# Two DeltaNet heads per scan and per substitution, with TensorE's order from an event list

## The chip, the core and the metric

The kernel runs on one core of one Trainium2 chip. The metric is the device time of one execution in microseconds (us). The engines are TensorE (PE, with its weight loads as PEld), VectorE (DVE), ScalarE (ACT), GpSimd (POOL) and SyncE (SP), whose queue issues the DMAs.

## The reference

One layer of a hybrid backbone over 512 latent tokens and 256 context tokens of width 1024: a half-step SwiGLU FFN, a token mixer, a second half-step FFN, a final norm. The mixer has two branches. The pooling branch forms windowed means of four channel groups. The gated DeltaNet branch has 8 heads of 128 channels; q, k and v come from one projection each, then a convolution of five taps over the tokens and SiLU. Each head is scanned in both directions in chunks, each with a decay and a beta of its own:

```python
def gdn_inputs(p, conv_w, a_log, dt_bias):
    qkv = short_conv(p[..., :QKV_END], conv_w).astype(jnp.float32)
    q, k, v = [t.reshape(B, L, GDN_HEADS, GDN_HEAD_DIM) for t in jnp.split(qkv, 3, axis=-1)]
    q = l2norm(q) * GDN_HEAD_DIM ** -0.5
    k = l2norm(k)
...
def gated_delta(q, k, v, beta, g, S0):
    cum = jnp.cumsum(gc, axis=-1)
...
    lmat = jnp.where(strict, jnp.einsum('nbhid,nbhjd->nbhij', kb, kc) * decay, 0.0)
    a_mat = lmat + jnp.eye(CHUNK, dtype=jnp.float32)
    rhs = jnp.concatenate([vb, kb * jnp.exp(cum)[..., None]], axis=-1)
    sol = lax.linalg.triangular_solve(a_mat, rhs, left_side=True, lower=True, unit_diagonal=True)
    aqk = jnp.einsum('nbhid,nbhjd->nbhij', qc, kc) * decay
...
    def step(S, xs):
        u_n, w_n, qd_n, kd_n, aqk_n, bl_n = xs
        v_new = u_n - jnp.einsum('bhcd,bhde->bhce', w_n, S)
        o = jnp.einsum('bhcd,bhde->bhce', qd_n, S) + jnp.einsum('bhij,bhje->bhie', aqk_n, v_new)
        S = S * bl_n[..., None, None] + jnp.einsum('bhcd,bhce->bhde', kd_n, v_new)
        return S, o
```

The latent scans start from the state at the end of the context's scan. The output of each head is normalised, gated and projected; a gated sum of both branches goes through one more projection.

## The kernel before

The kernel goes through four stretches: the first FFN, the pooling branch, the DeltaNet stage, and the merge with the second FFN. Dense products are made in three passes of half-width parts (`hi` and `lo` of weight and activation, line 132 in `job`); all small products take f32 operands directly, which the profile shows as two records for each matmul. Activations lie with channels on the partitions and 768 tokens (512 latent, 256 context) along the free axis, so a projection over both parts takes, for each of 8 input blocks and 3 passes, one matmul of 512 columns and one of 256. `weights` (L107) loads 512 KB of weights on SP's queue and splits them; `bank(tag)` (L51) hands out one of 8 banks of PSUM: 4 of `b` (projections), 2 of `g` (scan), 2 of `a` (the rest).

`head(h)` (L589) makes kf, qf and vf of one head: three `job`s, each followed by `conv_silu` (L567), which copies the projection from PSUM into `raw` with a border, scales the middle tap into `cv`, adds four taps on VectorE (L583) and applies SiLU. `head(0)` is called ahead of the pooling branch (L687), `head(1)` in the line behind it (L732). The pooling branch makes, for 2 halves and 4 token blocks, 24 matmuls of 256 columns into one bank and splits the result; then for 4 groups a window product and a small `job`. 

The DeltaNet stage has three generators a head. `front` (L757) transposes k into `kt` (L764), squares and sums it on ScalarE, transposes q for its norms (L771), and transposes v into `vt`. `invert` (L802) loads 2 rows of accumulated decay, broadcast to all partitions (`crow`, L808), forms exp(-|difference|) with 12 activations a head (L817), multiplies it into k times k (L824) as `L` and into k times q as `aqk`, and inverts the triangular matrices: blocks of 16 by forward substitution on VectorE, 15 steps of a product and a sum (L866) with `transpose`s around it (L872), then in three levels with small matmuls (L881 to L926). `scan` (L938) makes six chained steps, in each both directions of one head: state times k (L952), solve with `L`, state update with `kt` (L985), new state (L994). A step's two directions fill half a bank.

The loop at the end (L1038 on) runs scan of head k, inversion of head k+1 and front of head k+2 beside one another, in the order of letters in `ORDER`; behind each round stand the projections of head k+3, one output gate (`gate`) and a share of the 16 branch gates (`branch_gates`):

```python
    ORDER = "sfifsisiissiis"
    SHARE = (3, 2, 0, 0, 0, 0, 0, 0, 6, 5)
    for k in range(-2, H):
        stages = {c: g(i) for c, g, i in (("s", scan, k), ("f", front, k + 2), ("i", invert, k + 1)) if 0 <= i < H}
        for c in ORDER:
            if c in stages:
                next(stages[c], None)
...
        if k >= -1 and k + 3 < H:
            head(k + 3)
        if 0 <= k + 1 < H:
            gate(k + 1)
```

This text order is not the order of execution: a scheduler at build time orders each engine's instructions by its own estimates, within the data dependences. After the scheduling each engine takes its instructions in the given order.

Of the kernel before, what the change touches and what calls it, by code (L numbers as in the profile page):

```python
# [16 lines left out]
D = 1024  # L17
# [24 lines left out]
def layer_kernel(ctx, tc, a, out):  # L42
# [522 lines left out]
    kf, qf, vf = {}, {}, {}  # L565

    def conv_silu(w, tl, parts, dst, r=None):  # L567
        r = r or job(w, u_hi, u_lo, range(KT), parts)
        raw = pj.tile([128, 776], F32, tag="raw", name="raw", bufs=1)
        cv = pj.tile([128, 772], F32, tag="cv", name="cv", bufs=1)  # L570
        n = 772 if len(parts) == 2 else 512
        tap = [vec[:, 1, 24 * t + tl:24 * t + tl + 1] for t in range(5)]
        pool.memset(raw[:, 0:2], 0.0)
        pool.memset(raw[:, 514:518], 0.0)
        act.copy(out=raw[:, 2:514], in_=r["lat"][:, :512])
        act.activation(out=cv[:, 0:512], in_=r["lat"][:, :512], func=AF.Copy, scale=tap[2])
        if len(parts) == 2:
            pool.memset(raw[:, 774:776], 0.0)
            pool.memset(cv[:, 512:516], 0.0)
            act.copy(out=raw[:, 518:774], in_=r["ctx"][:, :256])  # L580
            act.activation(out=cv[:, 516:772], in_=r["ctx"][:, :256], func=AF.Copy, scale=tap[2])  # L581
        for t in (0, 1, 3, 4):
            dve.scalar_tensor_tensor(out=cv[:, :n], in0=raw[:, t:t + n], scalar=tap[t], in1=cv[:, :n],  # L583
                                     op0=ALU.mult, op1=ALU.add)
        act.activation(out=dst[:, 0:512], in_=cv[:, 0:512], func=AF.Silu)
        if len(parts) == 2:
            act.activation(out=dst[:, 512:768], in_=cv[:, 516:772], func=AF.Silu)

    def head(h):  # L589

        for c0, tl, parts, store, tag, bufs in ((D, 8, BOTH, kf, "kf", 4), (0, 0, ONLY, qf, "qf", 4), (2 * D, 16, BOTH, vf, "vf", 2)):
            store[h] = pj.tile([128, T if len(parts) == 2 else LAT], F32, tag=tag, name=tag, bufs=bufs)
            if h == 0 and c0 == D:
                conv_silu(None, tl, parts, store[h], res_k)
            else:
                conv_silu(weights(w_mix, 0, KT, c0 + 128 * h, EH), tl + h, parts, store[h])
# [135 lines left out]
    head(1)  # L732
# [4 lines left out]
    yg_dram = dr.tile([H, 128, LAT], F32, name="yg_dram")  # L737

# [7 lines left out]
    st = {}  # L746

    def g4(shape, name):
        return mp.tile(shape, F32, tag="g4", name=name, bufs=3)

    def s1(shape, name):
        return mp.tile(shape, F32, tag="s1", name=name, bufs=2)
# [3 lines left out]

    def front(h):  # L757

        kt = mp.tile([128, 6, 128], F32, tag="kt", name="kt", bufs=3)
        ss = mp.tile([128, 10], F32, tag="ss", name="ss", bufs=2)  # L760
        for c0, n in ((0, 4), (4, 2)):
            b = bank("a")
            for c in range(n):
                pe.transpose(b[:, c * 128:(c + 1) * 128], kf[h][:, (c0 + c) * 128:(c0 + c + 1) * 128], ident)  # L764
            act.copy(out=kt[:, c0:c0 + n].rearrange("p c x -> p (c x)"), in_=b[:, :n * 128])
            for c in range(c0, c0 + n):
                sq = mp.tile([128, 128], F32, tag="sq", name="sq", bufs=2)
                act.activation(out=sq, in_=kt[:, c], func=AF.Square, accum_out=ss[:, c:c + 1])
# [499 lines left out]
```

## Time and profile before

| | |
|---|---|
| median of 3 runs | 1755.21 us (1751.45, 1755.21, 1755.26) |
| profiled execution, its span | 1756.71 us, 1755.0 us |
| TensorE busy | 1653.5 us, 94% |
| its weight loads | 1423.9 us, 81% |
| VectorE, ScalarE, GpSimd busy | 1119.0, 842.6, 390.8 us |
| DMA | 183.82 MB, 105 GB/s on the mean |
| granted clock of TensorE, mean | 0.98 of 2.4 GHz |

Times in the rows are us from the span's start. The four stretches: first FFN to about 640, pooling to 722, DeltaNet stage to 1235, merge and second FFN from 1238 on. A row of the timeline names start, duration, engine, line, output, inputs, and in brackets the idle time ahead and what ended it. A group's row has its count, its total and mean duration, and the idle time of its engine ahead of it. TensorE is pipelined, so durations of single matmuls overlap; what a matmul costs is read from the distance of starts in a stretch without gaps.

### The profile page before, as it was taken

To read this page: it belongs to the slowest core of one execution; us is meant where nothing else is said; L and a number is where in the kernel's file an instruction comes from. 1 tells how busy PE (TensorE), PEld (TensorE's weight loads), DVE (VectorE), ACT (ScalarE), POOL (GpSimd) and SP (SyncE) were. 2 spreads that over 40 slices of the span, in tenths; PEclk is the share of its full clock that TensorE was granted. 3 is DMA by queue.
4 is the path that set the end of the run, shared out by engine and by line. 5 is a ranking of instruction groups with operands and counts; after the bars stand their busy time and mean duration, and the time that the engine had idled before them with its cause. 6 is when DMAs were issued, how large, how long until landed. Compare 5 with 4: busy or idle time off the path is not lost.

```text
span 1755.0 us, 31315 instructions
## 1 busy us (share of the span) xinstructions
PE 1653.5 (94%) x12220; PEld 1423.9 (81%) x12220; DVE 1119.0 (64%) x2254; ACT 842.6 (48%) x1851; POOL 390.8 (22%) x493
## 2 busy tenths in 40 slices
PE   6899999999999999889999999999998999999996
PEld 4889898989999778777878788787786788888885
DVE  5778888798888886375678767774555533333333
ACT  5443343434444364667677767665443322222233
POOL 2243444444454121123323331100000000000000
PEclk9999999999999999989999999999999999999998
DMA  9355536361221325532112212224654232333321
GB/s 273 112 155 151 156 96 182 103 189 65 78 67 56 108 82 187 138 100 67 44 52 65 60 45 53 56 61 154 214 158 116 69 98 88 94 96 96 93 64 48
DMA packets 282696, 183.82 MB, mean 105 GB/s; under 512 B 7008, under 2 KB 269877, under 8 KB 282421
## 3 DMA queue, kind: packets, MB, share of 16 engines
q1 hardware_dynamic: 282112, 181.65, 35.6%
q8 instruction: 96, 1.57, 0.4%
q14 instruction: 51, 0.42, 0.1%
q10 hardware_dynamic: 437, 0.18, 0.1%
HBM read 170.22 MB, written 11.58 MB: 104 GB/s over the span
## 4 chain that ended last, share of the span: by engine, by line
PE 71%; DVE 14%; ACT 5%; DMA 5%; POOL 2%; issue 2%; SPq 0%; ACTq 0%; POOLq 0%; DVEq 0%
PE b L132 22%; PE b L345 9%; PE a L132 6%; PE g L132 6%; PE a L345 5%; PE g L345 5%; DVE cv L583 2%; PE b L279 2%; PE a L279 1%; PE g L279 1%; PE a L708 1%; ACT din L848 1%; DVE wlo L120 1%; DMA bg_dram<-bgate 1%; PE b L150 1%
## 5 line engine op out<-in xcount | busy, mean ns | idle before, releaser
L188 ACT CAST fhi<-fst 128x512 fp32r<-128x512 f32 (+1 forms) x136 | 77.7, 605 | 249.6 <-PE b L132 85.6
L132 PE MATMUL b<-hhi,whi 128*128 128x512 f32 (+1 forms) x528 | 187.6, 384 | 0.0
L132 PE MATMUL b<-hlo,whi 128*128 128x512 f32 (+1 forms) x528 | 187.5, 383 | 0.0
L132 PE MATMUL b<-hhi,wlo 128*128 128x512 f32 (+1 forms) x528 | 186.9, 384 | 0.0
L179 POOL TENSOR_TENSOR rs<-rs,mhalf 128x4 f32<-128x4 f32 (+2 forms) x13 | 13.6, 1045 | 665.3 <-DVE rs L177 649.7
L189 DVE TENSOR_TENSOR flo<-fst,fhi 128x512 fp32r<-128x512 f32 (+1 forms) x136 | 87.3, 671 | 92.6 <-ACT fhi L188 92.4
L119 ACT CAST whi<-stg 128x512 fp32r<-128x512 f32 x146 | 89.4, 620 | 91.6 <-PE b L132 59.9
L119 ACT CAST whi<-qst 128x512 fp32r<-128x512 f32 (+1 forms) x160 | 81.6, 512 | 106.5 <-PE b L345 43.2
L119 ACT CAST whi<-qs 128x512 fp32r<-128x512 f32 (+1 forms) x120 | 59.5, 512 | 115.2 <-POOL qs L309 76.2
L583 DVE SCALAR_TENSOR_TENSOR cv<-raw,vec,cv 128x772 f32<-128x772 f32 (+1 forms) x96 | 101.6, 1058 | 11.6 <-ACT cv L581 8.3
L120 DVE TENSOR_TENSOR wlo<-qst,whi 128x512 fp32r<-128x512 f32 (+1 forms) x160 | 100.7, 639 | 10.1 <-ACT whi L119 10.0
L132 PEld LDWEIGHTS b<-hlo,whi 128*128 128x128 f32 x528 | 94.0, 190 | 14.8
L132 PEld LDWEIGHTS b<-hhi,whi 128*128 128x128 f32 x528 | 94.0, 190 | 14.8
L132 PEld LDWEIGHTS b<-hhi,wlo 128*128 128x128 f32 x528 | 93.3, 190 | 14.8
L308 POOL TENSOR_TENSOR qs<-qst 128x512 f32<-128x512 f32 (+1 forms) x40 | 46.4, 1161 | 247.2 <-DMA qst<-in_ffn_w_in_dram 76.6
L120 POOL TENSOR_TENSOR wlo<-stg,whi 128x512 fp32r<-128x512 f32 x46 | 65.4, 1430 | 90.6 <-ACT whi L119 70.6
L120 DVE TENSOR_TENSOR wlo<-stg,whi 128x512 fp32r<-128x512 f32 x100 | 68.2, 686 | 22.1 <-ACT whi L119 20.2
L188 ACT CAST ahi<-q 128x384 fp32r<-128x384 f32 x74 | 37.5, 512 | 75.4 <-DVE q L257 35.6
L120 DVE TENSOR_TENSOR wlo<-qs,whi 128x512 fp32r<-128x512 f32 (+1 forms) x80 | 49.0, 613 | 32.6 <-ACT whi L119 32.6
L132 PE MATMUL b<-xlo,fhi 128*128 128x512 f32 x160 | 63.4, 396 | 0.0
L132 PE MATMUL b<-xhi,flo 128*128 128x512 f32 x160 | 63.4, 396 | 0.0
L132 PE MATMUL b<-xhi,fhi 128*128 128x512 f32 x160 | 63.4, 396 | 0.0
(512 smaller groups left out, 4909.8 us busy)
## 6 DMA issues: line engine op xcount, KB each, us to landing
stg<-in_w_ada_dram SPq DMA_DIRECT2D x56, 512.0 KB, 4.0
stg<-in_w_mix_in_dram SPq DMA_DIRECT2D x49, 512.0 KB, 3.7
fst<-in_ffn_w_in_dram SPq DMA_DIRECT2D x44, 512.0 KB, 3.6
qst<-in_ffn_w_in_dram SPq DMA_DIRECT2D x40, 512.0 KB, 3.4
qst<-in_ffn_w_out_dram SPq DMA_DIRECT2D x40, 256.0 KB, 2.6
adx<-in_w_ada_dram SPq DMA_DIRECT2D x16, 512.0 KB, 6.4
fst<-in_ffn_w_out_dram SPq DMA_DIRECT2D x16, 512.0 KB, 3.9
crow<-cumd SPq DMA_DIRECT2D x16, 384.0 KB, 7.8
```

The costliest lines, as they stand in the source:

```text
L119: (first.copy if first is act else first.tensor_copy)(out=hi[:, :n], in_=w)
L120: second.tensor_tensor(out=lo[:, :n], in0=w, in1=hi[:, :n], op=ALU.subtract)
L132: pe.matmul(res[p][:, :m], lhsT=ww(i), rhs=hh(k)[:, o:o + m], start=(i == 0 and j == 0), stop=(i == n - 1 and j == 2))
L150: pe.matmul(b[32 * j:32 * j + 32, e * 128:(e + 1) * 128], lhsT=sc[:, k, :], rhs=stg[:, k, :], start=(i == 0), stop=(i == 1))
L188: act.copy(out=hi, in_=src)
L189: dve.tensor_tensor(out=lo, in0=src, in1=hi, op=ALU.subtract)
L279: pe.matmul(x, lhsT=ww(k), rhs=rhs(j, part, k), start=n + e == 0, stop=n + e == len(ks) + 1)
L308: pool.tensor_tensor(out=s1, in0=a21, in1=a22, op=ALU.add)
L345: pe.matmul(o, lhsT=ww[:, k], rhs=rhs(j, part, k), start=first and k + i == 0, stop=k + i == nh + 1, skip_group_check=not first)
L583: dve.scalar_tensor_tensor(out=cv[:, :n], in0=raw[:, t:t + n], scalar=tap[t], in1=cv[:, :n], op0=ALU.mult, op1=ALU.add)
L708: pe.matmul(r[:, :256], lhsT=hh[:, k, t * 128:(t + 1) * 128], rhs=ww[:, k], start=n == 0, stop=n == 3 * KT - 1)
L848: act.copy(out=din[o:o + 32, :, 0:12].rearrange("p f u -> p u f"), in_=L[o:o + 32, :, o:o + 32])
```

## The change

Heads are taken in four pairs. Each part of the stage is a generator that yields what it is about to use before it emits it: the engine, a cost in us written into the source, the buffers ("tokens") that it takes, and the events that it waits for. `run` keeps a clock for each engine and, of all threads, takes the one that could start first by these costs; what is emitted in that order is the kernel. On TensorE each instruction of the stage is kept behind the one emitted before it (`InOrder`); the other engines' instructions are still ordered by the scheduler.

What is computed in a pair at once: one substitution for both heads (24 matrices in the place of 12 in the same `[128, 32, 32]` tile), and one scan of six steps with two heads and two directions, which fill a bank. The products around the substitution stay per head. `L` and `aqk` of a head are written to DRAM (`l_dram`, `aq_dram`); each scan step loads its four 128 by 128 pieces back on SP's queue. The convolution reads the projection from PSUM, in two pieces, into its destination; `raw` and `cv` go. The norms of k are a wide square and a reduction on VectorE; those of q a wide square and four matmuls with a column of `ones`. Of a decay row, GpSimd forms the difference, and ScalarE takes Abs and Exp of 768 columns at once. `vt` is scaled on ScalarE. The call `head(1)` behind the pooling branch goes: head 1's projections are the first of the list's. Branch gates, output gates and projections are jobs of one `projections` thread with the lowest priority, whose weights are loaded ahead by two further threads.

```diff
-    def conv_silu(w, tl, parts, dst, r=None):
...
+    def conv_steps(tl, parts, r, dst):
+        tap = [vec[:, 1, 24 * t + tl:24 * t + tl + 1] for t in range(5)]
+        spans = [(r[p], PARTS[p][0], PARTS[p][1]) for p in parts]
+        def tap_of(x, o, n, t):
+            i0, i1 = max(0, 2 - t), n - max(0, t - 2)
+            d = dst[:, o + i0:o + i1]
+            dve.scalar_tensor_tensor(out=d, in0=x[:, i0 + t - 2:i1 + t - 2], scalar=tap[t], in1=d, op0=ALU.mult, op1=ALU.add)
+        for x, o, n in spans:
+            yield "act", n, lambda: act.activation(out=dst[:, o:o + n], in_=x[:, :n], func=AF.Copy, scale=tap[2])
...
-    head(1)
...
+    l_dram = [dr.tile([128, 12, 128], F32, name=f"l_dram{h}") for h in range(H)]
+    aq_dram = [dr.tile([128, 8, 128], F32, name=f"aq_dram{h}") for h in range(H)]
...
+    class InOrder:
+        def __getattr__(self, name):
+            return lambda *args, **kw: tc.keep_in_program_order(getattr(self.engine, name)(*args, **kw))
+    pe = InOrder(pe)
+    TOKENS = {"b": 4, "g": 2, "a": 2, "kf": FB["kf"] - 1, "qf": FB["qf"] - 1, "vf": FB["vf"] - 1, "kt": 4, "vt": 4, "dec": 3,
+              "L": 2, "g4": 3, "s1": 2, "tn": 1, "low": 1, "rv": 3, "S": 2, "ls": 2, "aqs": 1, "ot": 1, "yo": 2,
+              "sgate": 2, "stg": 2, "whi": WB, "wlo": WB}
...
+    def run():
+        while threads:
+            can = [(t, th["prio"], i) for i, th in enumerate(threads) for t in [start_of(th)] if t is not None]
+            t, _, i = min(can)
...
+    MM, TR = 0.2, 0.1
+    def projections():
...
+            for k in range(KT):
+                yield "pe", 0.69 + 0.36 * (len(parts) - 1), tags, (("w", j["name"], k // 4 * 4),)
+                hi, lo = j["w"][k // 4]
+                for e, (ww, hh) in enumerate(((hi, u_hi), (hi, u_lo), (lo, u_hi))):
+                    for p in parts:
+                        pe.matmul(r[p][:, :m], lhsT=ww[:, k % 4], rhs=hh(k)[:, o:o + m],
+                                  start=k + e == 0, stop=k + e == KT + 1)
...
+            spawn(j["then"](r), 0.5)
+    def qkv_job(h, i):
...
+        def then(r):
+            for e, n, emit in conv_steps(tl + h, parts, r, store[h]):
+                yield e, dcost(n) + 0.06 if e == "dve" else acost(n) + (0.06 if e == "act" else 0.0)
+                emit()
+                if e == "dve":
+                    last = state["end"]
+            done(f"{tag}{h}")
+            for _ in parts:
+                free_at["b"].append(last)
...
     def front(h):
+        for c0, n in ((0, 4), (4, 2)):
+            yield "pe", n * TR, ("a",)
...
+            yield "act", acost(n * 128)
             act.copy(out=kt[:, c0:c0 + n].rearrange("p c x -> p (c x)"), in_=b[:, :n * 128])
+            yield "act", acost(n * 128), ("yo",)
+            act.activation(out=sq[:, :n], in_=kt[:, c0:c0 + n], func=AF.Square)
+            yield "dve", dcost(n * 128)
+            dve.tensor_reduce(out=ss[:, c0:c0 + n], in_=sq[:, :n], axis=AX.X, op=ALU.add)
...
+    def front_q(h):
+        act.activation(out=sq, in_=qf[h], func=AF.Square)
         b = bank("a")
         for c in range(4):
-            pe.transpose(b[:, c * 128:(c + 1) * 128], qf[h][:, c * 128:(c + 1) * 128], ident)
+            pe.matmul(b[:, c:c + 1], lhsT=sq[:, c * 128:(c + 1) * 128], rhs=ones[:, 0:1])
...
+    def decay(h, d):
+        yield "sp", 0.05, ("dec",), ((f"own{h // 2 * 2 - 1}",) if h > 1 else ())
+        t = st[h]["dec", d] = mt([128, 6, 128], "dec", 3)
+        sp.dma_start(out=t, in_=cum_rows[d, h].partition_broadcast(128))
+        yield None, 3.5
+        yield "pool", 2.0
+        pool.tensor_tensor(out=t, in0=t, in1=bc(own, [128, 6, 128]), op=ALU.add)
+        yield "act", acost(768)
+        act.activation(out=tf, in_=tf, func=AF.Abs)
+        yield "exp", acost(768)
+        act.activation(out=tf, in_=tf, func=AF.Exp, scale=-1.0)
+        done(f"dec{h}{d}")
...
+    def substitution(p):
+        dve.transpose(out=au[:, 0:1024], in_=s["din"].rearrange("p a b -> p (a b)"))
...
+        dve.transpose(out=T_, in_=ti[:, 0:1024].rearrange("p (x y) -> p y x", y=32))
+        done(f"sub{p}")
+    def after(h):
...
+        yield "sp", 0.05
+        sp.dma_start(out=l_dram[h], in_=L)
+        give("L", 3.5)
+        done(f"inv{h}", 4.0)
+    def operands(p):
+        for s_ in range(6):
+            yield "sp", 0.1, ("ls",), evs
+            t = pair[p]["ls", s_] = mt([128, 2, 2, 128], "ls", 2)
+            for e in range(2):
+                sp.dma_start(out=t[:, e], in_=l_dram[2 * p + e][:, cf:6 + cb + 1:6 + cb - cf])
+            if s_ >= 2:
+                yield "sp", 0.1, ("aqs",)
...
+            done(f"ops{p}{s_}", 3.5)
+    def scan(p):
+        spawn(operands(p), 0)
+        UN = [(e, d) for e in range(2) for d in range(2)]
...
+                yield "pe", 4 * MM, ("g",)
+                for e, d in UN:
+                    pe.matmul(un(b, e, d), lhsT=kf[hs[e]][:, chunk[d] * 128:(chunk[d] + 1) * 128], rhs=S[:, e, d])
...
+            yield "pe", 4 * MM, ("g",), (f"ops{p}{s}",)
+            for e, d in UN:
+                pe.matmul(un(b, e, d), lhsT=ls[:, e, d], rhs=R[:, e, d] if s > 0 else vt[e][:, chunk[d]])
...
+    for p in range(H // 2):
+        for i in range(3):
+            for h in (2 * p, 2 * p + 1):
+                if h:
+                    qkv_job(h, i)
...
+    for p in range(H // 2):
+        spawn(pair_work(p), 2)
+    spawn(scans(), 0)
+    spawn(projections(), 6)
+    run()
```

## Rows read from the trace of the kernel before

**Rows 1.** page, part 1: engine, busy us (share of the span), number of instructions
```profile
PE 1653.5 (94%) x12220; PEld 1423.9 (81%) x12220; DVE 1119.0 (64%) x2254; ACT 842.6 (48%) x1851; POOL 390.8 (22%) x493
```

**Rows 2.** windows by stretch, columns in the first line
```profile
core 0: us, PE busy (x) PEld busy (x) DVE busy (x) ACT busy (x) POOL busy (x), PEclk, DMA share, GB/s
719.00:1238.00 519.00, 486.04 (x5454) 404.99 (x5452) 344.36 (x815) 356.66 (x928) 127.77 (x234) 0.99 0.28 76
...
1480.00:1520.00 40.00, 40.00 (x172) 32.15 (x171) 13.09 (x20) 8.48 (x15) 0.00 (x0) 1.00 0.32 94
...
692.00:702.00 10.00, 10.00 (x88) 10.00 (x88) 4.60 (x8) 1.75 (x4) 0.27 (x4) 1.00 0.21 55
...
745.70:752.30 6.60, 3.02 (x14) 3.02 (x15) 0.09 (x1) 5.26 (x25) 0.00 (x0) 0.50 0.56 144
```

**Rows 3.** timeline of TensorE at 923: start, us, engine, line, out<-in, records
```profile
922.80 1.06 PE L824 MATMUL a<-kf 128*128 128x128 f32 x8
923.69 0.61 PE L952 MATMUL g<-S,kf 128*128 128x128 f32 x4
```

**Rows 4.** timeline of TensorE at both ends of the stage
```profile
704.61 0.28 PE L132 MATMUL b<-hlo,whi 128*128 128x256 f32 x1
...
719.11 0.60 PE L764 MATMUL a<-ident,kf 128*128 128x128 f32 x4
...
722.40 0.39 PE L132 MATMUL g<-dh,pwl 128*128 128x512 f32 x1
...
1234.58 0.40 PE L132 MATMUL b<-hhi,wlo 128*128 128x512 f32 x1
...
1238.26 0.79 PE L132 MATMUL b<-yphi,whi 128*128 128x512 f32 x1 [3.28 <-ACT yphi L188]
```

**Rows 5.** TensorE groups by shape, 719 to 1238: busy us, mean ns, idle
```profile
L132 PE MATMUL b<-hhi,wlo 128*128 128x512 f32 x334 | 137.7, 412 | 0.0
...
L132 PE MATMUL b<-hlo,whi 128*128 128x256 f32 x96 | 29.5, 307 | 0.0
...
L952 PE MATMUL g<-S,kf 128*128 128x128 f32 x160 | 26.6, 289 | 5.6 <-DVE S L994 5.1 <-DVE tm L866 0.5
...
L881 PE MATMUL a<-tr,low 32*32 32x32 f32 x768 | 14.9, 235 | 4.8 <-DVE tr L872 4.7
...
L926 PE MATMUL a<-x,U 64*64 64x64 f32 x96 | 7.3, 222 | 0.0
```

**Rows 6.** waits of TensorE, 719 to 1238: total us, number, longest
```profile
PE a L771 <- ACT kt L765: 9.0, 1, 9.0
...
PE g L952 <- DVE S L994: 5.1, 6, 1.2
...
PE g L985 <- DVE vw L976: 3.8, 2, 2.0
```

**Rows 7.** window of line L132 alone: PE, PEld busy (records), PEclk, DMA share, GB/s
```profile
656.60:719.00 62.40, 29.97 (x142) 23.39 (x141) 0.97 0.51 166
```

**Rows 8.** DMA issues: queue, number, KB each, median us from issue to landing
```profile
crow<-cumd SPq DMA_DIRECT2D x16, 384.0 KB, 7.8
...
yg_dram<-y SPq DMA_DIRECT2D x8, 256.0 KB, 2.2
```

**Rows 9.** timeline of SyncE's queue and ScalarE, 726 to 750
```profile
727.37 1.01 SPq L808 DMA_DIRECT2D crow<-cumd  x2
...
735.81 1.86 ACT L817 ACTIVATE arg<-crow,ncumc 128x128 f32<-128x128 f32 x6 [4.03 <-DMA crow<-cumd]
```

**Rows 10.** ScalarE and VectorE groups by shape, 719 to 1238
```profile
L817 ACT ACTIVATE arg<-crow,ncumc 128x128 f32<-128x128 f32 x96 | 30.8, 398 | 7.0 <-DMA crow<-cumd 7.0
...
L872 DVE STREAM_TRANSPOSE tr<-ti 128x1024 f32<-128x1024 f32 x8 | 15.9, 1991 | 0.0
...
L866 DVE TENSOR_TENSOR tm<-au,ti 128x126 f32<-128x126 f32 x16 | 4.5, 284 | 0.2
...
L583 DVE SCALAR_TENSOR_TENSOR cv<-raw,vec,cv 128x772 f32<-128x772 f32 x52 | 62.2, 1197 | 8.4 <-ACT cv L581 8.0
```

More of the change, by code (lines that the diff above doesn't have):

```diff
@@ L589, in head @@
-    def head(h):
[L591 to L596, printed above, removed]
+    FB = {"kf": 5, "qf": 4, "vf": 2}
@@ new lines, in layer_kernel, with give, done, spawn @@
+    state = {"end": 0.0, "table": None}
+    events = {}
+    threads = []
+    def give(tag, after=0.0):
+        free_at[tag].append(state["end"] + after)
+    def done(name, after=0.0):
+        events[name] = state["end"] + after
+    def spawn(gen, prio):
+        th = {"gen": gen, "prio": prio, "t": state["end"], "last": "pe"}
+        threads.append(th)
+        step(th)
+    def step(th):
+        try:
+            w = next(th["gen"])
+        except StopIteration:
+            threads.remove(th)
+            return
+        th["want"] = (w[0], w[1], w[2] if len(w) > 2 else (), w[3] if len(w) > 3 else ())
@@ new lines, in start_of @@
+    def start_of(th):
+        e, cost, tags, evs = th["want"]
+        unit = "act" if e in ("exp", "silu") else e
+        t = th["t"] + (AFTER[th["last"]] if th["last"] and unit != th["last"] else 0.0)
+        for ev in evs:
+            if ev not in events:
+                return None
+            t = max(t, events[ev] + 0.2)
+        for tag in set(tags):
+            if len(free_at[tag]) < tags.count(tag):
+                return None
+            t = max(t, sorted(free_at[tag])[tags.count(tag) - 1])
+        return max(t, clock[unit]) if e else t
@@ L820, in invert, with before @@
+    def before(h):
+        s, p, e = st[h], pair[h // 2], h % 2
+        for d in range(2):
+            spawn(decay(h, d), 3)
+        yield None, 0.0, ("L",), (f"front{h}", f"dec{h}0", f"dec{h}1")
+        L = s["L"] = mt([128, 12, 128], "L", 2)
+        dec = [s["dec", d] for d in range(2)]
         for c0, n in ((0, 4), (4, 2)):
+            yield "pe", n * MM, ("a",)
             b = bank("a")
@@ L1055, in layer_kernel, with head_work, pair_work @@
-    assert not extra
+        give("yo", 2.5)
+        done(f"out{h}")
+    def head_work(h):
+        for g, prio in ((front(h), -1), (front_q(h), 1), (front_v(h), 2), (before(h), -1)):
+            spawn(g, prio)
+        yield None, 0.0, (), (f"front{h}",)
+    def pair_work(p):
+        if p:
+            yield None, 0.0, (), (f"din{2 * p - 1}",)
+        spawn(cleared(p), -1)
+        for h in (2 * p, 2 * p + 1):
+            spawn(head_work(h), -1)
+        yield None, 0.0, (), (f"din{2 * p}", f"din{2 * p + 1}", f"unit{p}")
+        spawn(substitution(p), -1)
+        for h in (2 * p, 2 * p + 1):
+            yield None, 0.0, (), (f"sub{p}",)
+            spawn(after(h), -1)
@@ L1056, in layer_kernel @@
+    gate_job(H - 2)
+    gate_job(H - 1)
+    for m in range(2 * KT):
+        branch_job(m)
+    for tag in ("kf", "qf", "vf"):
+        events[f"{tag}0"] = 0.0
+    for p in range(H // 2):
+        spawn(pair_work(p), 2)
+    spawn(scans(), 0)
+    spawn(projections(), 6)
+    run()
+    for h in range(H):
+        assert f"out{h}" in events
+    act, dve, pool, pe = engines
     mp_cm.__exit__(None, None, None)
```

669 lines of the change are left out of this document (472 added, 197 removed).

## The prediction

> **What bounds the kernel now.** I read the page's busy times first, then the windows by stretch, the groups of TensorE by shape inside the stretch that the change touches, its waits, and last the timeline at both ends of that stretch. The page says TensorE 94% busy [rows 1], but a matmul's end is modelled, so I count instructions instead. In the second FFN, where nothing interrupts it, 172 matmuls of 512 columns take 40.00 us, 0.2326 us each; in the pooling stretch 88 of 256 columns (and a few of 512) take 10.00 us, some 0.114 us each, and I use 0.1165, half of the former [rows 2]. Eight records of f32 matmuls of 128 columns take 923.69 - 922.80 = 0.89 us, 0.111 us a record [rows 3].
>
> The change touches the DeltaNet stage. Pooling's last matmul starts at 722.40, the first transpose of `front` at 719.11; the stage's last projection matmul starts at 1234.58, ends 0.23 later, and the merge begins at 1238.26 after a wait for ScalarE [rows 4]. In 719 to 1238 the groups hold 1001 matmuls of 512 columns (three groups of about 334, one shown) and 288 of 256 (three of 96): 232.8 + 33.6 us. Twelve groups of f32 matmuls and transposes (32 to 160 records, the largest shown) have 1088 records, 120.8 us. Seven groups of 32- and 64-row matmuls (L881 is the largest, L926 the smallest) are busy 75.8 us [rows 5]. That is 463 us; with some missing records I take 465. From 719.1 to 1234.8 are 515.7 us, so TensorE lacks work for about 51 us, a tenth. The stage is bound by TensorE; no other engine is near (VectorE 344, ScalarE 357, GpSimd 128 of 519 us [rows 2]). The waits say where part of the 51 us is: 9.0 once for `kt` at the start, 5.1 for the new state, 3.8 for `vw` [rows 6]; the rest is many short ones.
>
> A rule speaks for far more room. The weight loads are busy 405 of 519 us, 78% [rows 2]. The Trainium skill (Perfetto Trace Analysis, Identifying the Most-Contended Engine) calls matmul busy time a bad measure of headroom and weight-load busy time a good one. By that, some 114 us would be open here, and the sum below could fall by more than 60 us; but in the uninterrupted FFN stretch the same share is 32.15 of 40, 80%, so here the count decides and the trace does not bear the rule out.
>
> **The change part by part.**
>
> *TensorE's work.* The scan has the same matmuls for two heads in one bank instead of one head's in half a bank: 48 a head before and after. The substitution's small matmuls stay per head. Only the norms of q change: four transposes a head (one record each) become four f32 matmuls with `ones` (two records each): 8 x 4 x 0.111 = 3.6 us more. So none of the 465 us goes away; the change can win only from the 51 us of waiting.
>
> *Head 1 leaves pooling's shadow.* Before, head 1's three projections stand outside the stage and fill TensorE while pooling waits for its copies: L132 has 142 matmuls in 656.6 to 719 [rows 7], of which 5 finish head 0's v and 9 are pooling's own; the other 128 are head 1's k, q and v (72 of 512 and 48 of 256 columns, 16.7 + 5.6 us) and 8 of a branch gate (1.9), together 24.2 us. The blocks between two pooling products are such a filling, as the one at 704.61 [rows 4]. After, head 1 is in the event list, and every TensorE instruction of the list is kept behind the one traced before it, the first behind pooling's last matmul. Pooling's own chain (a copy, eight products, a copy) does not get shorter without the filling, so these 24.2 us move behind 722.6. From below this costs nothing if pooling ends that much earlier, from above 24.2; I take 24.2, since in the trace the products resume as soon as the copy is done.
>
> *Start of the list.* The second batch of k's transposes is listed after the first batch's copy, square and reduction, and the projections stand behind it: some 3 us idle. The first decay rows are counted with 3.5 us in the list; the row load lands after 7.8 us [rows 8], and before, ScalarE waited 4.03 us for it after the issue at 727.37 [rows 9]. The first score matmul waits behind it, and all fill listed later waits too, since TensorE takes no other order: 4 us, between 0 and 9 (the present wait [rows 6]). I take 7 us for the start against the present 9 and more, which goes because head 1's projections fill it.
>
> *Steady state.* Without the start the 51 us leave some 40 us of short waits, 8%. For the change: the substitution runs once for a pair, so of VectorE's 8 transposes of 1991 ns 4 go, with 4 each of the two shorter ones, and half of the 240 little products and sums of some 0.26 us, 31 us (one group of them shown) [rows 10]; ScalarE loses the 96 activations of 398 ns [rows 10] against 32 wide ones, and the tap copies of the convolution (the taps, 1.2 us for 772 columns now [rows 10], read PSUM in two pieces); 24 chained scan steps take the place of 48. Against it: the list fixes the order by written-in costs, and where a copy or a load is later than listed, TensorE stands though other work is ready. The projection loop's banks are held until the last tap is done. I bound the waits by 8% of 492 us (40) and 2% (10) and take 20, near half of the present 8%, as both other busy engines are relieved.
>
> *Through DRAM.* L goes out in one DMA of 768 KB a head and comes back step by step, 80 loads on SP's queue in all, behind which weight loads queue, and the step's solve product waits for them. The trace has a 256 KB write with 2.2 us and the 384 KB rows with 7.8 [rows 8]; so 2.2 to 7.8 us each way. The pair's chain has projections of the next pairs to hide it as long as these last (290 us of them); I count nothing, and up to 4 x 8 = 32 us if the cover is gone. The Trainium skill (DMA: Bandwidth & Descriptors, Anatomy of one DMA) gives a fixed 2 us or so per transfer, nearly all of it the receipt of the last write, which by its formula makes 3.8 us for 768 KB; the 2.2 us row agrees with it, the 7.8 us row does not.
>
> *Clock.* After the 9 us wait the granted clock is 0.50 in 745.7 to 752.3 [rows 2], the 1.2 GHz level. Pooling without its filling has idle stretches of 2 to 11 us; a stretch at that level of the length shown costs 3.3 us. I count it into the 7 us and keep 3 us for the range. The Trainium skill (TensorE: Matmul & The Clock Gate, HAM oscillation) warns of idle gaps between short bursts in the same sense; by it (an estimate) pooling would end 2 to 4 us later.
>
> *Sum.* Start 722.6; work 465 - 1.2 (pooling's last five) + 24.2 + 3.6 = 491.6; start 7; waits 20; the gap to the merge 3.4 as now: 722.6 + 491.6 + 7 + 20 + 3.4 = 1244.6, against 1238.3: 6.3 us later. What follows is unchanged. The profiled execution has a span of 1755.0 us and took 1756.7; the median of the three runs is 1755.2. The sum is made on the span, which is the median within 0.2 us: **1761.5 us**.
>
> **The rivals.**
>
> *The list orders so well that waits nearly vanish (faster).* Waits of 2% (10 us) with a start of 3: 1244.6 - 14 = 1230.6, 7.7 us earlier, 1747. With no wait at all 1217.6, 1734, is the floor. For it: the list's cost of a projection step, 0.69 us, is that of three matmuls of 0.2326, and the chains have slack. It decides from 18 us of waiting in all downwards.
>
> *TensorE stands behind late operands (slower).* One mechanism: a fixed order meets a DMA or a VectorE queue later than listed. The second head of each pair needs a row load after the first one's scores; 7.8 against 3.5 us is 4.3 us, four times 17, and DRAM reads behind SP's queue as much again: 1761.5 + 17 to 34 = 1778 to 1795. Against: other work of the list lies between.
>
> *The order isn't pinned where it matters.* If head 1's projections still run in pooling's shadow, 24.2 us come back: 1737.
>
> *The counted f32 work is itself waiting.* The 197 us of f32 and small matmuls are counted at the rate they show; if a third of that were latency that wider batches hide, the stage would shrink by 60 us: 1700. For it: the rule above of the Trainium skill (Perfetto Trace Analysis, Identifying the Most-Contended Engine), which would find its room here. Against: the eight records of [rows 3] follow each other without a wait at that rate.
>
> **How the numbers follow.** Forecast (20 to 40 us of start and waits, 1754 to 1774) 0.47; nearly no waits 0.25; standing behind operands 0.20; not pinned 0.05; latency in the f32 work 0.03. A measurement tells 0.3%, 5.3 us, from no change. Faster takes the second, fourth and fifth cases less a little, 0.31; same is the lower half of the forecast's band and the upper edge of the second, 0.26; slower is the other half and the third, 0.43. The range leaves 0.1 on each side: 1737 to 1788; the forecast's own is 1754 to 1774.
>
> **What would show it.** Right: between pooling's first product and its last, TensorE has idle blocks of some 2 us where L132 stood, and L132 begins after pooling's last matmul; in the stage the same counts of records; the merge starts near 1245. VectorE's L872-like transposes number 4. Wrong: projections inside pooling's stretch; a waiting total (515.7 us against the counted work) over 45 or under 18 us; a rate of the f32 records other than 0.111 us; waits of TensorE that name the L or score tiles from DRAM.

## The result and the profile after

The changed kernel takes 1838.48 us (median of 4 runs, 1835.82 to 1839.63), the kernel before 1754.66 beside it: ratio 1.0479, 95% interval 1.0461 to 1.0498. Forecast were 1761.5 us, with 1737 to 1788 as the range. The direction was right; the loss is 84 us where the forecast had 6.

First the page's busy times, then the windows of the profiled execution (span 1837.9 us), cut where pooling's last product and the merge's first start; columns as in [rows 1, 2].

```profile
PE 1667.6 (91%) x12252; PEld 1450.2 (79%) x12252; DVE 1089.5 (59%) x2187; ACT 780.8 (42%) x1515; POOL 401.8 (22%) x432
```

```profile
640.00:721.40 81.40, 60.83 (x326) 52.22 (x326) 32.53 (x79) 37.14 (x50) 4.38 (x10) 0.79 0.41 130
721.40:1321.40 600.00, 513.99 (x5609) 446.01 (x5607) 328.21 (x746) 303.91 (x613) 148.51 (x191) 0.90 0.35 102
...
800.00:820.00 20.00, 7.64 (x413) 7.14 (x415) 11.21 (x26) 4.14 (x10) 4.61 (x10) 0.50 0.11 29
1321.40:1837.90 516.50, 495.48 (x2114) 396.66 (x2114) 209.93 (x330) 166.94 (x291) 2.01 (x2) 0.98 0.34 100
```

The whole loss lies in the DeltaNet stage. Behind the merge 516.5 us are left, and before they were 1755.0 - 1238.3 = 516.7; ahead of 721.4 nothing was lost in sum. The stage takes 600.0 us in the place of 515.9 (722.4 to 1238.3, [rows 4]). TensorE is busy 514 us of it, about 31 more than before, and idle 86, where [rows 2] show 519.0 - 486.0 = 33 for nearly the same stretch. VectorE and ScalarE are less busy than before, with 328 and 304 us against 344 and 357; GpSimd is busier, with 149 against 128, and far from full.

What TensorE waits for in the stage, as in [rows 6] (total, times, longest), and the groups that carry the added work, as in [rows 5]:

```profile
PE a L760 <- DVE tr L1157: 30.9, 3, 17.3
PE a L760 <- issue: 15.5, 12, 2.1
PE b L132 <- ACT yphi L188: 7.5, 1, 7.5
PE g L760 <- DVE S L1362: 6.4, 1, 6.4
PE g L760 <- DMA ls<-l_dram: 5.5, 4, 3.0
```

```profile
L760 PE MATMUL b<-hhi,whi 128*128 128x512 f32 x360 | 158.1, 439 | 0.0
...
L760 PE MATMUL b<-hhi,whi 128*128 128x256 f32 x112 | 32.4, 289 | 2.8 <-DVE kf L576 2.8
...
L760 PE MATMUL a<-tr,low 32*32 32x32 f32 x768 | 14.8, 244 | 37.4 <-DVE tr L1157 30.9 <-issue 6.5
...
L760 PE MATMUL a<-ones,yo 128*128 128x1 f32 x64 | 7.9, 244 | 0.8 <-ACT yo L1008 0.7
```

Line 760 is the wrapper that pins TensorE's order, so every instruction of the stage bears it. Three groups of 360 are 1080 matmuls of 512 columns (1001 before), three of 112 are 336 of 256 (288 before). The wait for the transposes behind the substitution (`tr`) was 4.7 us for eight heads [rows 5]; it is 30.9 for four pairs.

The largest wait, on five queues (start, duration, engine, line, output and inputs, and what the engine waited for):

```profile
783.12 0.39 SPq L1042 DMA_DIRECT2D dec<-cumd  x1
...
791.49 1.48 POOL L1046 TENSOR_TENSOR dec<-dec,ncumc 128x768 f32<-128x768 f32 x1 [6.66 <-PE b L760]
...
786.16 0.69 ACT L578 ACTIVATE qf<-b,vec 128x512 f32<-128x512 f32 x1
793.00 0.84 ACT L1049 ACTIVATE dec<-dec 128x768 f32<-128x768 f32 x1 [6.16 <-POOL dec L1046]
...
788.10 0.26 DVE L1147 TENSOR_TENSOR tm<-au,ti 128x110 f32<-128x110 f32 x1
788.28 0.74 DVE L576 SCALAR_TENSOR_TENSOR kf<-b,vec,kf 128x510 f32<-128x510 f32 x1
788.95 0.26 DVE L1150 TENSOR_TENSOR ti<-ti,tm 128x110 f32<-128x110 f32 x1
...
799.06 0.75 DVE L576 SCALAR_TENSOR_TENSOR qf<-b,vec,qf 128x510 f32<-128x510 f32 x1 [4.43 <-ACT qf L578]
...
806.96 1.86 DVE L1157 STREAM_TRANSPOSE tr<-ti 128x1024 f32<-128x1024 f32 x1
...
791.29 0.38 PE L760 MATMUL a<-ident,kf 128*128 128x128 f32 x2
808.96 2.44 PE L760 MATMUL a<-tr,low 32*32 32x32 f32 x133 [17.30 <-DVE tr L1157]
```

VectorE alternates a step of the substitution (L1147, L1150) with a tap of a convolution (L576). The list has the 30 small steps and the two transposes behind them in one piece, 15 x (0.28 + 0.27) + 1.25 + 2.0 = 11.5 us by its written-in costs (14 with the transpose ahead of them and what stands between); here they go from 781.87 to 808.82, 27 us. Into this falls a standstill: a decay row is issued at 783.12 and GpSimd adds to it at 791.49 (the bracket names a TensorE matmul as what ended that wait; that it was the row is read from its issue 8.4 us before, where the stage's rows take a median of 7.0), ScalarE stands 6.16 us in front of it, and the tap scaling behind it (`qf`, L578) holds VectorE for 4.43. TensorE, whose next instruction in the list is the product behind the substitution, waits 17.3 us, and then works at a granted clock of 0.50 from 800 to 820.

### The profile page after: what moved, and what is told of

It is laid out like the page before. It is cut to its first block, busy times and chain, and to the rows that moved or that the text cites. A ratio compares the mean times of both kernels' runs of the same rounds, so it can differ in the third digit from the quotient of the medians.

```text
span 1837.9 us, 31100 instructions
## 1 busy us (share of the span) xinstructions
PE 1667.6 (91%) x12252; PEld 1450.2 (79%) x12252; DVE 1089.5 (59%) x2187; ACT 780.8 (42%) x1515; POOL 401.8 (22%) x432
## 4 chain that ended last, share of the span: by engine, by line
PE 74%; DVE 10%; DMA 6%; ACT 4%; issue 3%; POOL 2%; SPq 1%; POOLq 0%; ACTq 0%; DVEq 0%
PE b L132 13%; PE b L760 13%; PE b L345 8%; PE a L132 6%; PE g L132 6%; PE g L345 5%; PE a L345 5%; PE a L760 5%; PE g L760 4%; PE b L279 2%; DMA dec<-cumd 2%; PE a L706 1%; PE a L279 1%; PE g L279 1%; DVE xT L437 1%
## 5 line engine op out<-in xcount | busy, mean ns | idle before, releaser
L760 PE MATMUL b<-hhi,whi 128*128 128x512 f32 x472 | 172.3, 404 | 2.8 <-DVE kf L576 2.8
L760 PE MATMUL b<-hlo,whi 128*128 128x512 f32 x472 | 159.5, 377 | 0.0
L760 PE MATMUL b<-hhi,wlo 128*128 128x512 f32 x472 | 159.2, 376 | 0.0
L760 PEld LDWEIGHTS b<-hhi,wlo 128*128 128x128 f32 x472 | 83.7, 194 | 16.7
L760 PEld LDWEIGHTS b<-hhi,whi 128*128 128x128 f32 x472 | 84.2, 196 | 15.3 <-issue 3.3
L760 PEld LDWEIGHTS b<-hlo,whi 128*128 128x128 f32 x472 | 84.5, 196 | 12.8
L877 POOL TENSOR_TENSOR wlo<-stg,whi 128x512 fp32r<-128x512 f32 x37 | 47.6, 1286 | 182.9 <-ACT whi L872 182.4
L872 ACT CAST whi<-stg 128x512 fp32r<-128x512 f32 x90 | 55.1, 617 | 70.1 <-PE b L760 61.5
L877 DVE TENSOR_TENSOR wlo<-stg,whi 128x512 fp32r<-128x512 f32 x53 | 36.2, 687 | 63.3 <-ACT whi L872 63.2
L437 DVE SCALAR_TENSOR_TENSOR xT<-q,eff,xT 128x128 f32<-128x128 f32 (+2 forms) x100 | 64.1, 661 | 0.1
L132 PE MATMUL b<-xhi,flo 128*128 128x512 f32 x160 | 63.4, 396 | 0.0
L132 PE MATMUL b<-xlo,fhi 128*128 128x512 f32 x160 | 63.4, 396 | 0.0
L132 PE MATMUL b<-xhi,fhi 128*128 128x512 f32 x160 | 63.4, 396 | 0.0
```

Source lines behind the costliest of these rows:

```text
L132: pe.matmul(res[p][:, :m], lhsT=ww(i), rhs=hh(k)[:, o:o + m], start=(i == 0 and j == 0), stop=(i == n - 1 and j == 2))
L437: dve.scalar_tensor_tensor(out=r[:, o0:o1], in0=c[i][j][:, o0 - j * n2:o1 - j * n2], scalar=gate(m + i, s), in1=r[:, o0:o1], op0=ALU.mult, ...
L760: return lambda *args, **kw: tc.keep_in_program_order(getattr(self.engine, name)(*args, **kw))
L872: act.copy(out=hi, in_=stg[:, i:i + 4])
L877: eng.tensor_tensor(out=lo, in0=stg[:, i:i + 4], in1=hi, op=ALU.subtract)
```

## The experiments

Theory A: the change pins TensorE to the list's order and leaves VectorE, ScalarE and GpSimd to the scheduler, and the two orders don't fit. Theory B: the list has 3.5 us for a decay row that takes 7 to 8, and all queues stand behind it. Theory C is on the waits that the profile puts down to `issue`; D and E ask whether TensorE's work or the chain of pairs sets the pace. All times are medians, with the kernel before at 1752.8 to 1756.3 beside them.

**Orders.** Every engine in the list's order, and none:

```diff
-    pe = InOrder(pe)
+    act, dve, pool, pe = (InOrder(e) for e in (act, dve, pool, pe))
```


> Theory A (two orders): TensorE follows the event list, but VectorE, ScalarE and GpSimd follow the scheduler, which mixes the substitution with convolution taps, so that it takes 27 us where the list has 14; with every engine kept in the list's order the waits of 17.3 and 11.5 us for the transposes behind the substitution fall to under 3 and the time to 1795 to 1810. Theory B (late decay rows): the list believes in 3.5 us for a row load that takes 7 to 8, and ScalarE's queue stands behind it; keeping more engines in the list's order changes nothing on that or makes it worse: 1830 to 1855.

Measured 1805.57 (1802.94 to 1806.57), 33 less than the changed kernel. The second kernel only takes the line `pe = InOrder(pe)` out:

> The list's order as text order only, TensorE free. Theory A: the scheduler's orders fit each other again, TensorE's waits of over 0.3 us sum to 35 to 55 us instead of 85: 1785 to 1805. Theory B: the row loads are as late for the scheduler's own order, the 6 us waits of ScalarE for them stay and TensorE has no more work ready than now: 1825 to 1840.

Measured 1789.31 (1784.12 to 1797.94). In the first, VectorE's order and TensorE's wait, and the waits of the stage:

```profile
794.96 0.19 DVE L760 TENSOR_TENSOR tm<-au,ti 128x30 f32<-128x30 f32 x1
795.48 3.07 DVE L760 STREAM_TRANSPOSE tr<-ti 128x1024 f32<-128x1024 f32 x2
...
798.70 1.54 PE L760 MATMUL a<-tr,low 32*32 32x32 f32 x80 [3.01 <-DVE tr L760]
```

```profile
PE a L760 <- issue: 14.8, 13, 2.1
PE g L760 <- DMA ls<-l_dram: 10.8, 4, 4.8
...
PE a L760 <- DVE tr L760: 4.9, 2, 3.0
```

The wait for `tr` falls from 30.9 to 4.9 us, as A has it. Which engine is it? TensorE pinned with one other:

```diff
-    pe = InOrder(pe)
+    dve, pe = InOrder(dve), InOrder(pe)
```
The other run has `act` in the place of `dve`.

> TensorE and VectorE in the list's order, ScalarE and GpSimd in the scheduler's. Theory A as first told (VectorE's mixing of substitution and taps is the mismatch): most of the 33 us that pinning all engines gave, 1803 to 1815. Theory B: ScalarE's place behind the decay rows is it: 1825 to 1845.

> TensorE and ScalarE in the list's order, VectorE and GpSimd in the scheduler's. Theory A as first told: the waits for the transposes behind the substitution stay at 25 to 35 us, 1828 to 1845. Theory B: 1803 to 1818.

Measured 1838.58 and 1833.19: neither alone gives much, 5.3 us at most. With VectorE pinned the substitution runs in one piece, and ScalarE still stands in front of the decay row:

```profile
801.98 3.05 DVE L760 STREAM_TRANSPOSE tr<-ti 128x1024 f32<-128x1024 f32 x2
...
803.42 0.84 ACT L1049 ACTIVATE dec<-dec 128x768 f32<-128x768 f32 x1 [6.53 <-POOL dec L1046]
```

The waits of the whole stage tell the two causes apart. First come ScalarE's waits for decay rows (`dec`) in the changed kernel, then both waits with VectorE pinned, both with ScalarE pinned, and ScalarE's with all pinned:

```profile
ACT dec L1049 <- POOL dec L1046: 50.0, 11, 7.8
...
ACT dec L1049 <- POOL dec L1046: 55.6, 12, 7.4
PE a L760 <- DVE tr L760: 3.5, 1, 3.5
...
ACT dec L760 <- POOL dec L1046: 11.0, 3, 8.2
PE a L760 <- DVE tr L1157: 27.4, 3, 13.2
...
ACT dec L760 <- POOL dec L760: 11.4, 5, 7.5
```

Each of the two runs takes most of one wait away, keeps the other, and gains little; with all pinned both are small, and 33 us are gone. With VectorE pinned TensorE's idle time in the stage does fall, from 86 to 592.6 - 522.2 = 70 us, but its busy time is 8 us longer and the stage starts 5 us later (726.4); the waits for L, the output and the state are 7.7, 7.0 and 6.5 us for 4.1, 3.7 and 6.4. So "VectorE's mixing" as first told fell, and so did ScalarE's standing in front of decay rows on its own: with no engine pinned ScalarE waits 45.5 us for rows, TensorE 2.9 for `tr`, and the time is 1789. What stays of A is that the engines' orders must fit each other. Whether three engines without GpSimd would do wasn't tried.

**Late rows.** The listed latency 3.5 becomes 9.0, in the changed kernel and with all engines pinned:

```diff
-        yield None, 3.5
+        yield None, 9.0
         yield "pool", 2.0
```


> Only the listed latency of the decay rows changes, 3.5 to 9 us. Theory A: the mixing on VectorE stays, so the waits for the transposes stay within 5 us: 1825 to 1840. Theory B: ScalarE's waits of 6 to 7.5 us for a decay row go, and with them the wait of 6.4 for the new state and most of the 17.3: 1805 to 1818.

> All engines in the list's order, the decay rows listed with 9 us in the place of 3.5. Theory B, now where the list sets every order: ScalarE and GpSimd no longer stand in front of a row, 5 to 15 us less, 1790 to 1800. Rival: the row loads are late but not on the path, and the first pair starts later: 1803 to 1820.

Measured 1856.43 (18 more than the changed kernel) and 1818.18 (1803.29 to 1821.72, 13 more than with all pinned). The first doesn't test B: ScalarE's order is the scheduler's, and its waits for rows stay at 49.5 us. The second does: they fall from 11.4 to 0.7 us, and nothing is gained. With the runs above, B as the main cause fell.

**Head 1's projections** stand ahead of the stage again, with TensorE pinned, with none, with all. The list then has one buffer fewer of `kf`, `qf` and `vf`:

```diff
+    head(1)
     mp_cm = tc.tile_pool(name="mp", bufs=1, reuse_waits="tile")
...
-                if h:
+                if h > 1:
                     qkv_job(h, i)
...
```


> Head 1's three projections stand again ahead of the stage, where they can run beside pooling; the list begins with both heads of the first pair made. The prediction's term: 24.2 us of TensorE's work leave the stage, 1810 to 1818. Rival: pooling's own chain grows by as much, or the first pair waits elsewhere: 1828 to 1840.

> The list as text order only, and head 1's projections ahead of the stage. If TensorE's work bounds the stage when its order is the scheduler's, the 24.2 us of the prediction come back here: 1789 - 24 = 1765 (1760 to 1772). If waits decide as in the pinned order, 1782 to 1792.

> All engines in the list's order, head 1's projections ahead of the stage. Theory D: with orders that fit, TensorE's work bounds the stage, so the 22.3 us of matmuls that leave it come off: 1805.6 - 22 = 1783 (1776 to 1790). Theory E: the chain of pairs (substitution, products around it, scan) sets the pace and TensorE's work is fill, as the 2 us of the same edit with mixed orders say: 1798 to 1810.

Measured 1836.09, 1820.77 and 1785.05. With TensorE alone pinned the stage has 72 matmuls of 512 and 48 of 256 columns fewer and nothing is gained: TensorE idles 101 us in it for 86, with 27.2 us for `tr` and 16.9 for the state. With none pinned the projections went into pooling's shadow anyway, and yet the time is 31 us longer; the list is another one, and no run separates what else it does. With all pinned 20.5 us come off, as D has it; the nudged list below shows why one such difference isn't enough.

**Runs of tiny matmuls.** Between two blocks of 96 records of 32-row matmuls the list must place a projection step (a token that `apart` gives back after a step, or after 3 us without one); first with all pinned, then with head 1 outside too:

```diff
-        yield "pe", 1.9, ("a",)
+        yield "pe", 1.9, ("a", "apart")
+        spawn(apart(), 7)
...
```


> All engines in the list's order, and after each block of 96 records of 32-row matmuls at least one step of a projection before the next such block. Theory C (a long run of tiny matmuls outruns what feeds TensorE with instructions): the 14.8 us of waits for nothing that the profile shows fall to under 4, the time by 8 to 15 us to 1790 to 1798. Rival: these waits are semaphores that the profile doesn't resolve; they stay, 1800 to 1812.

> All engines in the list's order, head 1 outside, and a projection step between two blocks of tiny matmuls. Theory C (runs of tiny matmuls outrun their supply): the 14.4 us of waits for nothing in the profile fall to under 5 and are not given back now that orders fit: 1785 - 9 = 1776 (1770 to 1780). Rival: the second head's products come later and the pair with them: 1781 to 1792.

Measured 1802.55 and 1811.31. The waits called `issue` fall from 14.8 to 6.0 and from 14.4 to 8.7 us. They were to fall under 4 and 5, but the direction bears C out on what makes them. The time doesn't follow: the second head's products come later, and waits for `tr` (12.0 and 12.7) and for L from DRAM (13.9 in the latter) take their place.

**SyncE's queue** in the list's order too, with all pinned and head 1 outside, without and with the blocks apart:

```diff
-    engines = act, dve, pool, pe
+    engines = act, dve, pool, pe, sp
+    sp = InOrder(sp)
```


> As the run with all engines in the list's order and head 1 outside, and SyncE's queue in the list's order too. Theory A in its widest form (any queue in another order than the list costs): the waits for loads and for ScalarE's splits of weights go, 1770 to 1780. Rival: a queue in the list's order stands behind stores whose data come late, and weight loads behind them: 1785 to 1800.

> Both together. If each takes off what its theory says, 1760 to 1772; if the list itself is what is left, 1775 to 1795. Under 1750 it would beat the kernel before.

Measured 1802.79 and 1824.86, 18 and 40 more than the 1785 us of the kernel with all pinned and head 1 outside. Nothing is gained, so A in its widest form has no support here; the times lie above the rival's 1785 to 1800 and the combination's 1760 to 1795 too, and no run shows that late stores cause them.

**How far can an edit of the list be read?** In the kernel of 1785 us every listed VectorE cost gets 0.01 us more; in another the listed costs that the traces contradict are mended:

```diff
-        return 0.2 + 0.00095 * n
+        return 0.21 + 0.00095 * n
```

```diff
-    MM, TR = 0.2, 0.1
+    MM, TR = 0.228, 0.1
...
-        yield None, 3.5
-        yield "pool", 2.0
+        yield None, 7.3
+        yield "pool", 1.5
...
-            done(f"ops{p}{s_}", 3.5)
+            done(f"ops{p}{s_}", 5.0)
```


> All engines in the list's order and head 1 outside (1785 us), and one written-in cost changed by almost nothing: every listed VectorE operation is 0.01 us longer. If an edit of the list does what it says, 1783 to 1787. If the list is a greedy order that any change shuffles, the time jumps by as much as in the runs with blocks apart, 10 us or more either way.

> As the run with all engines in the list's order and head 1 outside, with the three listed costs that the traces contradict: an f32 matmul 0.228 in the place of 0.2, a decay row 7.3 in the place of 3.5 (GpSimd's addition 1.5 in the place of 2.0), the loads of a scan step 5.0 in the place of 3.5. If false costs are what is left of the waits, 1765 to 1778; if the list scatters whatever it is told, anything from 1775 to 1815.

Measured 1801.87 (1798.22 to 1813.62) and 1811.67. An edit that says nothing costs 17 us: the greedy list falls into another order, and any single difference of under some 17 us between two lists shows nothing on its cause. This is one nudge, so the scatter may be larger; the two kernels with none pinned are 31 us apart. By this measure head 1's 20.5 us is barely told apart, and late rows, blocks apart and measured costs are not settled by their times. What is above it are groups: the five kernels that pin TensorE with at most one other engine take 1833 to 1856 us, the seven that pin all four engines (SyncE free) 1785 to 1818, with no overlap.

Stronger still are kernels with the same list. Pinning changes no written-in cost, so the order in which the instructions are emitted stays, and the scatter between lists is out of these pairs: TensorE's order in the traces is the same within a pair to 98% or more, and to 53% between the kernel of 1785 us and the nudged one. TensorE alone against all four engines is 1838 against 1806 in the list as changed, 1856 against 1818 with the latency of 9, 1836 against 1785 with head 1 outside: 33, 38 and 51 us, each time the same way.

**The convolution from PSUM** alone, put into the kernel before (`conv_steps` of the change in `head`, `conv_silu` gone):

```diff
-                conv_silu(weights(w_mix, 0, KT, c0 + 128 * h, EH), tl + h, parts, store[h])
+                r = job(weights(w_mix, 0, KT, c0 + 128 * h, EH), u_hi, u_lo, range(KT), parts)
+            for _, _, emit in conv_steps(tl + h, parts, r, store[h]):
+                emit()
```


> The kernel before with one part of the change: the convolution reads PSUM in two pieces and works in its destination. Relief of ScalarE (two copies fewer a projection) against more pieces on VectorE and banks held until the last tap: TensorE's waits hardly change, 1748 to 1757. Rival: held banks stall the projections, 1757 to 1770.

Measured 1755.39, ratio 1.0020 (1.0004 to 1.0036): no gain. In its stage ScalarE is busy 333 us for some 355, and TensorE's idle time is no smaller (34 us, in its longest execution of 1762.59).

No kernel beat the one before; the best of the others, all engines pinned with head 1 outside, is 1.74% behind it (1.0152 to 1.0196).

## Why the prediction was wrong, point by point

**What bounds the kernel:** right for the kernel before. The stage had 33 us of visible waits, so there was little to win and much to lose. One reading was wrong: there are eight groups of 32- and 64-row matmuls, not seven, and the 75.8 us lack this one:

```profile
L905 PE MATMUL a<-x,U 32*32 32x32 f32 x384 | 9.7, 194 | 0.0
```

With it the count is some 475 us and the present lack 41. The forecast would have come out up to 10 us later, at 1772, still 67 us short.

**TensorE's work:** right. 79 more matmuls of 512 columns and 48 of 256 are 79 x 0.2326 + 48 x 0.1165 = 24.0 us, for a term of 24.2. The q norms were put at 3.6 us more: 64 `ones` records are busy 7.9 us, and the 32 transposes that went were 3.6 by the 0.11 us a record of [rows 3], so the term is right within 1 us. The f32 records of 128 columns still start 0.111 us apart at the full clock (the median of 980).

**Head 1 leaves pooling's shadow:** right in the sum, by luck in the second half. In pooling the filled blocks are now idle, and its last product starts at 721.18, 1.2 us earlier, not 24:

```profile
704.59 0.63 PE L720 MATMUL a<-win,phi 128*128 128x512 f32 x1
705.02 0.63 PE L720 MATMUL a<-win,plo 128*128 128x512 f32 x1
707.68 0.50 PE L720 MATMUL a<-win,phi 128*128 128x512 f32 x1 [2.03 <-ACT win L716]
...
721.18 0.39 PE L132 MATMUL g<-dh,pwl 128*128 128x512 f32 x1
```

But this hides two effects. These windows go from pooling's first product to its last, in the changed kernel, in the kernel before, and with all pinned and head 1 outside:

```profile
664.20:721.20 57.00, 44.68 (x236) 38.53 (x237) 13.40 (x18) 16.62 (x20) 2.89 (x9) 0.76 0.36 121
...
672.60:722.40 49.80, 49.78 (x315) 44.40 (x316) 24.15 (x32) 25.77 (x40) 0.51 (x7) 0.97 0.41 140
...
665.50:713.90 48.40, 46.88 (x306) 41.61 (x306) 23.43 (x37) 20.57 (x28) 1.79 (x6) 1.00 0.41 129
```

Pooling starts 8.4 us earlier, as it also does with head 1 back (665.5) and with the convolution from PSUM alone (665.8), so this isn't the missing filling. And it takes 7.2 us longer, with fewer matmuls, at a lower granted clock (the rows at 704.59 and 705.02 above start 0.43 us apart, for 0.23 at the full clock). With head 1 back it takes 48.4 us at the full clock. So the filling cost pooling nothing, and its absence 7 to 9 us.

**Start of the list:** right in size, not in its parts. Waits of 0.7 (norms of q), 2.6 (a score product) and 2.8 us (a bank held by a tap) up to 750 make 6.1, for 7; the second batch of transposes waits for nothing.

**Steady state: the step that failed.** The waits of the steady state were put at 20 us. The profile shows 86 us of idle time; without the start (6.1) and the gap to the merge (7.5) these are 72, where the kernel before has 33 - 9.0 - 3.3 = 21. By the prediction's own measure, the stage's time less the counted work, the whole is 600.0 - 491.6 = 108 us for 30, far over the 45 that it named as a sign of being wrong. The 2% and 8% by which I bounded the waits were the present kernel's ratio and less, for a mechanism that I named only as a rival: in the kernel before all engines' orders come from one scheduler. I took relief of VectorE and ScalarE as fewer waits for TensorE. Both are relieved (16 and 53 us less busy) and TensorE idles 53 us more. The upper bound should have come from the fact that the diff pins one engine of four. What that is worth is shown by the same list with all four pinned: 33 us less time, and 570.3 - 513.9 = 56 us of idle time for 86. Of the 23 us of idle time that it still has over the kernel before, most stands as `issue` (14.8, none before), L from DRAM (10.8) and the gap to the merge (5.7 for 3.3); no run took all of these away.

**Through DRAM:** nothing was counted, up to 32 us if the cover is gone. TensorE waits 5.5 us for it, and up to 13.9 where products come later. The write itself is short: the DMA issues of the changed kernel have 3.2 us for its 768 KB, near the 2.2 of [rows 8]. The estimate from the Trainium skill (DMA: Bandwidth & Descriptors, Anatomy of one DMA) was 3.8; the formula stands there for transfers issued by GpSimd, and these are SyncE's.

**Clock:** a term that was too small, in both places. In pooling the granted clock is 0.76 from the first product to the last, and pooling takes 7.2 us longer; the estimate by the Trainium skill (TensorE: Matmul & The Clock Gate, HAM oscillation) had 2 to 4 us later, and the trace agrees with its direction. In the stage the clock is at 0.50 (1.2 GHz) for 121 us, for 11 before; it falls in or right behind the long waits, as in the one of 17.3 us. A step of one matmul of 512 columns and one of 256 then starts 0.64 us after the last one, and 0.35 at the full clock:

```profile
743.20:753.40 10.20, 7.42 (x27) 6.18 (x26) 8.58 (x17) 4.15 (x6) 4.25 (x6) 0.50 0.32 105
...
748.61 0.84 PE L760 MATMUL b<-hhi,wlo 128*128 128x512 f32 x2
749.25 0.84 PE L760 MATMUL b<-hhi,whi 128*128 128x512 f32 x2
...
755.13 0.51 PE L760 MATMUL b<-hlo,whi 128*128 128x512 f32 x2
755.48 0.51 PE L760 MATMUL b<-hhi,wlo 128*128 128x512 f32 x2
```

At the lower level the trace has 49 matmuls of 512 columns (0.43 us each), 20 of 256 and 67 f32 records of 128 (0.21 each). That is some 18 us more than at the full clock, for 3 before, where the prediction kept 3 for the range. The busy time rose by 31 us all the same, not by 24 + 4 + 15; that short pauses inside the busy time became fewer is the likely remainder, not measured.

**The rivals:** "TensorE stands behind late operands" happened, with a chance of 0.20, but not by its trigger alone. The decay row of 7.8 us listed as 3.5 is in the trace at 783 to 793; yet ScalarE's waits for rows go with ScalarE pinned, and 1833 us stay. Its price of 17 to 34 us counted late loads one by one and not orders that don't fit; TensorE's idle time grew by 53. "Waits nearly vanish" needed all orders to agree, and even in the best of those kernels TensorE idles 55 of 553 us. "Not pinned where it matters": in the kernel with nothing pinned 67 of head 1's 72 wide matmuls do go into pooling's shadow, and it is the fastest with head 1 in the list. "The counted f32 work is itself waiting" fell: the rate of 0.111 us a record stayed in the wider batches.

**Weight loads:** by the rule of the Trainium skill quoted there (Perfetto Trace Analysis, Identifying the Most-Contended Engine) room would have been 22% before and is 26% now (446 of 600 us). More room beside more waiting doesn't speak against the rule; what does is the share of 80% in the FFN stretch without a gap [rows 2].

What stays open: why the kernels with all orders in one piece are still 30 to 65 us behind. Named are 24 us of moved work, the waits for instructions, and the lower clock behind all waits (some 20 us by the same count with all pinned); that any of them would come back in full was not shown, since an edit of the list that says nothing moved the time by 17 us.

## What to carry to other kernels

An order written by hand for one engine is only as good as the orders of the engines that feed it: pin all that exchange data or none, and when a diff pins one, don't take its waits from a kernel whose orders come from one scheduler. Before reading an edit of a greedy list, nudge a cost that means nothing and see how far the time moves. A gain in a busy share of an engine that isn't the bound is no gain. Work taken out of another stage's shadow costs its full length, and the stage that it leaves can slow down too: here pooling took 57.0 us for 48.4 to 49.8.

## What the runs showed of the hardware

The waits that the profile calls `issue` go with the supply of instructions. After 133 records of tiny matmuls in 2.4 us TensorE stops, with one packet of the queue of kind `instruction` in the stretch around it and nothing else (DMA view of 809.8 to 812.6):

```profile
808.96 2.44 PE L760 MATMUL a<-tr,low 32*32 32x32 f32 x133 [17.30 <-DVE tr L1157]
812.59 1.19 PE L760 MATMUL a<-tr,low 32*32 32x32 f32 x58 [1.18 <-issue]
```

```profile
DMA packets 1, 0.02 MB, mean 6 GB/s; under 512 B 0, under 2 KB 0, under 8 KB 0
...
q8 instruction: 1, 0.02, 2.8%
```

In the traces of the changed kernel and the sixteen experiments there are 133 such waits of over 0.3 us from pooling on, and all end 2.2 to 3.2 us after a packet of that queue began; the stage's 44 packets come 14 us apart on the mean. The kernel before has the same blocks of 96 records and 96 such packets, and not one such wait: larger matmuls stand between its blocks, where the changed kernel has up to 672 small records in a row. In the nudged run one of these waits lasts 10.17 us, and in the ten us (1097.3 to 1107.3) other loads (two decay rows were issued at 1091.5) keep the DMA engines busy nearly half the time; the packet that ends it began only 2.4 us before:

```profile
1107.37 0.26 PE L761 MATMUL a<-U,x 32*32 32x32 f32 x1 [10.17 <-issue]
```

```profile
q1 hardware_dynamic: 1245, 0.61, 46.1%
q8 instruction: 1, 0.02, 0.6%
```

That the row loads held the packet back is suggested by this, not shown.
